# First modulation in two halves of the channels, the loads of the start reordered, and five products in two parts

## The chip, the cores and the metric

One core of one Trainium2 chip runs the whole kernel, one launch of it. The metric is the time on the device in microseconds, the median over runs. Before the change it is 1413.9 us over 3 runs (1413.7 to 1414.58).

## The reference, cut to what matters

A two-layer transformer on 512 tokens of 1024 channels, with a context of 256 tokens. Layer 0 is attention with a mixture of experts, layer 1 a pooling mixer with another one. What the change touches is the beginning of layer 0: a vector of conditions is multiplied by a wide matrix, w_ada (1024 x 6144 per layer), and gives shifts, scales and gates; the normalised input is scaled and shifted by them and goes through one projection to queries, keys and values.

```python
cond_lat, cond_ctx = jax.nn.silu(c), jax.nn.silu(c_ctx)
mod_l = (cond_lat @ w_ada[i] + b_ada[i])[:, None, :]
sh_m, sc_m, g_m, sh_f, sc_f, g_f = jnp.split(mod_l, 6, axis=-1)
h_l = modulate(rms_norm(x_lat, norm_mix_g[i]), sh_m, sc_m)
mc = jnp.split(cond_ctx @ w_ada[i] + b_ada[i], 6)
h_c = modulate(rms_norm(x_ctx, norm_mix_g[i]), mc[0], mc[1])
qkv = h_l @ w_qkv
q_l = rope(rms_norm(q, q_g)); k_l = rope(rms_norm(k, k_g))
kv_c = h_c @ w_qkv[:, 1024:]
```

## The kernel before, in words

Every engine's instructions stand in the order in which the Python code issues them; no scheduler reorders them. The start of the kernel is one function, `project`.

**The stream of weights.** `plan_stream` lists the weight loads in their order, and `Stream.fill` issues them on SyncE's queue (L118) while fewer than `limit` tiles are out and a buffer of the shared pool of 22 is free. `Stream.get` takes a tile, `Stream.done` returns it and fills again. SyncE's queue is one sequence: each load waits for the eighth load before it.

**The first modulation.** The columns 0 to 2047 of w_ada are the shift and the scale of the first norm. They come as eight tiles of 128 rows by 2048 columns, 1 MB each. `ada_part` (L354) multiplies one by the two condition vectors: four matmuls, one for each 512 columns, on the four column groups of TensorE. After 32 of them `ada_rows` holds rows of results (L361), `ada_place` turns them (L441), so that channels lie on partitions, and adds the bias and the norm's gain (L455, L457).

**The normalised input.** `square` and `scale` (L600 to L609) normalise the two context tiles and then the four tiles of x. `h_turn` (L631) turns 128 channels of them on TensorE into a bank, `h_make` applies the modulation on ScalarE (L648) and parts the result in two fp32r numbers, `hi` by a cast on VectorE (L649) and `lo` by a subtraction (L650), on VectorE or POOL by the chunk. `weight_parts` parts the projection's weights in the same way (`split`, L519 on ScalarE and L520 on VectorE or POOL).

**The products.** `seq` has 14 of them, 128 tokens by 512 columns each: 0 and 1 are keys and values of the context, 2 to 5 keys and values of x, 6 to 13 queries. A product is 24 matmuls (`matmul3`, L546): eight chunks of channels by three combinations of parts. Products 0 and 1 need the context's h and the column block 2 of the weights, product 2 all eight chunks of x's h.

**What follows a product.** `others(n)` is called after product n. On VectorE and ScalarE, `turned` takes the norm of product n-1's heads (sum of squares L699, root, several small steps, L702) and applies the rope (L711, with L708 on POOL); between its steps `parted` makes the parts of product n-2's heads (L718, L519, L520), and two steps of `work` part weights of the next column block. Then `place` turns the heads of product n-2 on TensorE (L740), and ScalarE copies them out in the next round (L753). Since TensorE takes its instructions in order, product n+1 stands behind the turns of product n-2, and these behind VectorE's parts.

In the profile `pmm` is a product, `hTc` and `hT` the parts of h for the context and for x, `whl` the parts of the weights, `hl` those of the heads, `ph` the turned input, `pqt` the turned heads, `wt` a tile of the stream.

Of the kernel before, what the change touches and what calls it, by code (L numbers as in the profile page):

```python
# [178 lines left out]
class Kernel:  # L179
# [88 lines left out]
    def plan_stream(self):  # L268
# [12 lines left out]
        ada(0, 0)  # L281
        qkv(2)
# [47 lines left out]
    def cond_columns(self, ps):  # L330
        nc = self.nc
        nc.scalar.activation(self.rowsA[0:16], self.rowsA[0:16], AF.Silu)
        p = ps.tile([128, 512], F32, tag="tr", name="pc")
        nc.tensor.transpose(p[:, :96], self.rowsA, self.ident[:96, :96])
        nc.vector.tensor_copy(self.cols[:, :96], p[:, :96])
        self.cond = self.cp.tile([128, KD, 32], F32, name="cond")
        nc.vector.memset(self.cond, 0.0)
        for c in range(2):
            nc.vector.tensor_copy(self.cond[:, :, c], self.cols[:, 8 * c:8 * c + 8])

# [91 lines left out]
    def ada_place(self, i, b, rows, ps, tag="tr", no_dve=False):  # L432
        nc = self.nc
        eng = nc.gpsimd if no_dve else nc.vector
        if b:
            q = slice(64 * (b - 1), 64 * b)
            eng.tensor_tensor(self.gates[q], self.gates[q], rows[q], op=ALU.add)
        p = ps.tile([128, 512], F32, tag=tag, name="pa")
        pv = p.rearrange("p (n j c) -> p n j c", n=4, c=32)
        for n in range(4):  # L440
            nc.tensor.transpose(p[:, n * 128:(n + 1) * 128], rows[:, n * 128:(n + 1) * 128], self.ident)  # L441
        gains = {1: self.cols[:, 16 + 8 * i:24 + 8 * i], 4: self.cols[:, 32 + 8 * i:40 + 8 * i]}
        tv = lambda z: z.rearrange("p (j n) -> p n j", j=2)
        for m in (2 * b, 2 * b + 1):
            if m in (2, 5):
                continue
            for cond in range(2 if (i == 0 and m < 2) else 1):
                t = self.cp.tile([128, KD], F32, name=f"mod{i}{m}{cond}")
                j0 = 2 * (m % 2)
                bias = self.cols[:, 48 + 48 * i + 8 * m:56 + 48 * i + 8 * m]  # L450
                src = pv[:, :, j0:j0 + 2, cond]
                if no_dve:
                    nc.scalar.copy(tv(t), src)
                    src = tv(t)
                eng.tensor_tensor(tv(t), src, tv(bias), op=ALU.add)  # L455
                if m in gains:
                    nc.vector.scalar_tensor_tensor(t, t, 1.0, gains[m], op0=ALU.add, op1=ALU.mult)  # L457
                self.AB[i, m, cond] = t
# [80 lines left out]
    def matmul3(self, p, lhs, whl, half=None):  # L539

        n = 0
        for k in range(KD):
            if half and k == KD // 2:
                half()
            for pa, pb in ((0, 0), (0, 1), (1, 0)):
                self.nc.tensor.matmul(p, lhs(pa, k), whl[pb, k // 4][:, k % 4], start=(n == 0), stop=(n == 3 * KD - 1))  # L546
                n += 1

    def attention_layer(self, sa):
# [7 lines left out]
        with ExitStack() as s1:  # L557
            self.ps3 = Banks(pool(s1, "psP", 1, space=PSUM), {"mm": 3, "tr": 3})
# [8 lines left out]
    def project(self, s1):  # L567
# [19 lines left out]
        self.gate_biases(0, nc.sync)  # L587
# [22 lines left out]

        js = (4, 5)
# [10 lines left out]
        def h_turn(cond, k):  # L622
# [3 lines left out]
            else:  # L626
                if k % 2 == 0:
                    ph["c"] = ps3.tile([128, 512], F32, tag="mm", name="ph") if k < 6 else ps.tile([128, 512], F32, tag="o", name="ph")
# [5 lines left out]
        def h_make(cond, k):  # L634
# [15 lines left out]
            (nc.vector if k % 4 < 2 else nc.gpsimd).tensor_tensor(lo, h32, hi.bitcast(F32), op=ALU.subtract)  # L650

        for k in range(KD):
            h_turn(1, k)
        for _ in range(4 * KD):
            self.ada_part()
        whl, work = self.weight_parts("qkv", 2, engs=(nc.vector, nc.gpsimd))
        js = range(NT)
        ss = sm.tile([128, NT], F32, name="ss4")
        for _ in range(4):
            work.popleft()()  # L660
        self.ada_end(ps3)
        for part in range(2):
            hT[part, 2] = self.big([128, KD, CTX], F32R, "hTc")
        for z in range(4):
            h_make(1, 2 * z)
            for _ in range((0, 1, 1, 2)[z]):
                work.popleft()()
            if z >= 2:
                square(js, 2 * z - 4, nc.scalar, ss)
                square(js, 2 * z - 3, nc.vector, ss)  # L670
        r = self.rstd_of(ss, NT, D, "n4")
        for j, eng in enumerate((nc.scalar, nc.gpsimd, nc.vector, nc.gpsimd)):
            scale(js, j, eng, r)
# [3 lines left out]
        def product(ch, j, whl, half=None):  # L677

            p = self.ps3.tile([128, 512], F32, tag="mm", name="pmm")
            if j < NT:  # L680
                self.matmul3(p, lambda z, k: hT[z, k // 4][:, k % 4, j * 128:(j + 1) * 128], whl, half)
            else:
                self.matmul3(p, lambda z, k: hT[z, 2][:, k, (j - NT) * 128:(j - NT + 1) * 128], whl, half)
# [71 lines left out]
        def make_tabs():  # L755

            nc.gpsimd.tensor_copy(self.tri_b, rest[:, :128])
            p = ps3.tile([128, 512], F32, tag="tr", name="pc")
            nc.tensor.transpose(p[:, :48], rows1, self.ident[:48, :48])
            nc.vector.tensor_copy(self.cols[:, 96:], p[:, :48])  # L760
            nc.gpsimd.tensor_scalar(gq[:, 0], gq[:, 0], HD ** -0.5, 0.0, op0=ALU.mult, op1=ALU.add)
            for i, n in ((1, "k"), (0, "q")):
                tcs = tabs[n]
                nc.gpsimd.tensor_tensor(tcs[:, 0], rope[:, 0], gq[:, i][:, None, :].to_broadcast([128, NT, HD]), op=ALU.mult)
                for e in range(2):
                    nc.gpsimd.tensor_tensor(tcs[:, 1, :, e::2], rope[:, 1, :, e::2],
                                            gq[:, i, 1 - e::2][:, None, :].to_broadcast([128, NT, HD // 2]), op=ALU.mult)

# [21 lines left out]
        def chunks(turns, makes=()):  # L790
            for k in turns:
                h_turn(0, k)
            for k in makes:
                h_make(0, k)

        work = deque()
        for n, (ch, j) in enumerate(seq):
            if n in (0, 6, 10):
                while work:
                    work.popleft()()  # L800
                whl, (nxt, work) = whl if n == 0 else nxt, self.weight_parts("qkv", 0 if n == 0 else 1) if n < 10 else (None, deque())
            half = {1: lambda: chunks((3, 4, 5), range(3))}.get(n)
            P1[n] = ch, j, product(ch, j, whl, half)
            if n == 0:
                chunks(range(3))
            if n == 1:
                chunks((6, 7), range(3, 8))
                make_tabs()
            others(n, work if n != 1 else None)
# [939 lines left out]
```

## Time and profile before

| | us |
|---|---|
| median of 3 runs | 1413.9 |
| the profiled execution | 1411.9 |
| its span | 1410.1 |
| TensorE busy in it | 1318.7 (94%) |
| VectorE busy | 667.9 (47%) |
| ScalarE busy | 372.7 (26%) |
| GpSimd (POOL) busy | 179.7 (13%) |
| moved by DMA | 474.92 MB, mean 337 GB/s |
| first matmul of product 0 | 35.92 after the span's start |
| first matmul of product 13 | 135.54 |

A timeline row gives an instruction's start, its duration (of all `xcount` merged ones from the first start to the last end), the engine, the line and the operation, tiles as out<-in, and in brackets how long the engine had been idle and what ended that. A window's row gives the busy time of PE, PEld, DVE, ACT and POOL, the granted clock of TensorE as a share of full speed, the DMA engines' busy share, and GB/s. PE is TensorE, PEld its weight load, DVE VectorE, ACT ScalarE, SP SyncE.

### The profile page before, as it was taken

The numbers are of one execution on the slowest core, as the hardware profiler recorded it, in microseconds if no ns is written. First come the engines' busy times: TensorE is split into PE (matmuls) and PEld (weight loads), VectorE is DVE, ScalarE is ACT, GpSimd is POOL, SyncE is SP. The second block draws the span as 40 slices with busy tenths as digits, with TensorE's granted clock in tenths as the row PEclk, the third lists the DMA queues.
The fourth block names the chain that finished last, engine by engine and source line by source line (L and its number), as shares of the span: only waits on it lengthen the run. The fifth ranks groups of instructions, "written<-read, shape, count | busy, mean of one in ns | idle before, by whom it ended". The sixth has DMA issues, their size and how long they took to land. (4 is left out here: it accounts for less than half of the span.)

```text
span 1410.1 us, 18553 instructions
## 1 busy us (share of the span) xinstructions
PE 1318.7 (94%) x7135; PEld 742.5 (53%) x7135; DVE 667.9 (47%) x1241; ACT 372.7 (26%) x713; POOL 179.7 (13%) x159
## 2 busy tenths in 40 slices
PE   4799999998699999999999997779999999999995
PEld 1588677777544554445444444554444544455432
DVE  2777788757433343334342337733433433343325
ACT  2454678744310111111110114511101101011103
POOL 1523254454100000000000014300000000000001
PEclk8899999999899999999999999989999999999998
DMA  9412844178379999999999999458999999999993
GB/s 376 154 61 72 346 156 173 51 266 330 122 286 421 427 426 427 426 426 427 427 426 426 423 417 418 164 198 368 426 426 426 426 427 426 427 427 426 426 420 147
DMA packets 80410, 474.92 MB, mean 337 GB/s; under 512 B 8478, under 2 KB 10030, under 8 KB 30140
## 3 DMA queue, kind: packets, MB, share of 16 engines
q1 hardware_dynamic: 80308, 473.66, 82.0%
q8 instruction: 59, 0.97, 0.3%
q14 instruction: 35, 0.29, 0.1%
q10 hardware_dynamic: 8, 0.01, 0.0%
HBM read 471.54 MB, written 2.10 MB: 336 GB/s over the span
## 5 line engine op out<-in xcount | busy, mean ns | idle before, releaser
L1239 PE MATMUL pgate<-wt,xe 128*64 128x512 f32 x1024 | 264.1, 593 | 0.0
L1239 PE MATMUL pup<-wt,xe 128*64 128x512 f32 x1024 | 263.8, 592 | 0.0
L1264 PE MATMUL py<-wt,aT 128*64 128x512 f32 x960 | 212.6, 595 | 0.0
L1244 DVE TENSOR_TENSOR act<-act,pup 128x512 f32<-128x512 f32 x32 | 22.1, 690 | 335.1 <-ACT act L1243 299.7
L1295 DVE TENSOR_TENSOR x<-x,pc 128x512 f32<-128x512 f32 x240 | 154.1, 683 | 33.0 <-PE pc L1293 33.0
L1222 PE MATMUL pga<-OH,xnp 128*128 128x256 f32 x1024 | 146.5, 290 | 11.1 <-issue 11.1
L1239 PEld LDWEIGHTS pup<-wt,xe 128*64 128x64 f32 x1024 | 74.7, 137 | 145.1 <-issue 144.8
L1222 PEld LDWEIGHTS pga<-OH,xnp 128*128 128x128 f32 x1024 | 138.8, 196 | 19.9 <-issue 12.9
L1239 PEld LDWEIGHTS pgate<-wt,xe 128*64 128x64 f32 x1024 | 74.0, 137 | 142.5 <-issue 132.9
L1293 PE MATMUL pc<-y,scat 128*128 128x512 f32 x480 | 136.6, 405 | 2.5 <-DVE x L1295 2.5
L1277 DVE SCALAR_TENSOR_TENSOR py<-py,r_sw,gw 128x512 f32<-128x512 f32 x64 | 48.6, 759 | 177.4 <-PE py L1264 168.5
L1264 PEld LDWEIGHTS py<-wt,aT 128*64 128x64 f32 x960 | 66.9, 137 | 124.7 <-issue 118.5
L1243 ACT ACTIVATE act<-pgate 128x512 f32<-128x512 f32 x32 | 19.1, 597 | 366.2 <-PE pgate L1239 366.2
L1293 PEld LDWEIGHTS pc<-y,scat 128*128 128x128 f32 x480 | 80.5, 188 | 43.4 <-ACT act L1243 24.3
L1278 ACT ACTIVATE y<-py 128x512 fp32r<-128x512 f32 x64 | 38.2, 597 | 236.8 <-PE py L1264 175.8
L1228 ACT ACTIVATE xe<-pga,mod 128x256 f32<-128x256 f32 x64 | 36.2, 565 | 167.7 <-PE pga L1222 165.3
L546 PE MATMUL pmm<-whl,hT 128*128 128x512 f32 x288 | 70.0, 399 | 0.0
L837 DVE TENSOR_REDUCE mx<-S 128x1 f32<-128x768 f32 x64 | 58.3, 951 | 19.6 <-PE S L834 18.9
L1701 POOL TENSOR_TENSOR xg<-x,gn 128x512 f32<-128x512 f32 x4 | 5.0, 1275 | 479.5 <-DVE x L1327 479.5
L546 PEld LDWEIGHTS pmm<-whl,hT 128*128 128x128 f32 x288 | 54.1, 191 | 11.1
L1226 DVE TENSOR_SCALAR xe<-pga,mod 128x256 f32<-128x256 f32 x64 | 34.8, 544 | 48.3 <-PE pga L1222 44.8
L844 ACT ACTIVATE P<-S,mx 128x768 f32<-128x768 f32 x64 | 57.0, 899 | 2.2 <-POOL rest L718 2.0
(327 smaller groups left out, 1457.5 us busy)
## 6 DMA issues: line engine op xcount, KB each, us to landing
wt<-in_moe_w_gate_up_dram SPq DMA_DIRECT2D x224, 1024.0 KB, 16.1
wt<-in_moe_w_down_dram SPq DMA_DIRECT2D x120, 1024.0 KB, 12.7
wt<-in_w_ada_dram SPq DMA_DIRECT2D x48, 1024.0 KB, 14.2
wt<-in_moe_w_gate_up_dram SPq DMA_DIRECT2D x64, 512.0 KB, 10.3
wt<-in_moe_w_down_dram SPq DMA_DIRECT2D x16, 512.0 KB, 10.5
wt<-in_attn_w_qkv_dram SPq DMA_DIRECT2D x6, 1024.0 KB, 7.4
x<-in_x_dram SPq DMA_DIRECT2D x8, 512.0 KB, 7.9
wt<-in_attn_w_o_dram SPq DMA_DIRECT2D x4, 1024.0 KB, 5.6
```

The costliest lines, as they stand in the source:

```text
L546: self.nc.tensor.matmul(p, lhs(pa, k), whl[pb, k // 4][:, k % 4], start=(n == 0), stop=(n == 3 * KD - 1))
L837: nc.vector.tensor_reduce(m, s[:, :NKEY], axis=AX, op=ALU.max, negate=True)
L844: nc.scalar.activation(P[n][:, g], S.pop((n, g))[:, :NKEY], AF.Exp, bias=mx[n, g], accum_out=total[n // 4][:, 2 * gp + g, kvl:kvl + 1])
L1222: nc.tensor.matmul(p[:, :n], self.parts[part][j // 2][:, j % 2, k * 128:(k + 1) * 128], OH[:, j], start=(z == 0), stop=(z == 2 * NT - 1))
L1226: nc.vector.tensor_scalar(xe, p[:, :n], A[:, k:k + 1], B[:, k:k + 1], op0=ALU.mult, op1=ALU.add)
L1228: nc.scalar.activation(xe, p[:, :n], AF.Identity, bias=B[:, k:k + 1], scale=A[:, k:k + 1])
L1239: nc.tensor.matmul(p[64 * e:64 * e + 64], xe(k)[:, off + 64 * e:off + 64 * e + 64], w[e][:, h * 512:(h + 1) * 512], start=(k == 0), stop=( ...
L1264: nc.tensor.matmul(py[h][64 * e:64 * e + 64], aT[:, j, 64 * e:64 * e + 64], wd[e][:, h * 512:(h + 1) * 512], start=(j == 0), stop=(j == 3) ...
L1277: nc.vector.scalar_tensor_tensor(py, py, w, gf[:, h * 512:(h + 1) * 512], op0=ALU.mult, op1=ALU.mult)
L1278: nc.scalar.activation(y[:, 0], py, AF.Copy)
L1293: nc.tensor.matmul(p, P[:, j * 128:(j + 1) * 128], y[:, part], start=(part == 0), stop=(part == 1))
L1295: nc.vector.tensor_add(xs, xs, p)
```

## The change

The order of the loads: x, rope tables and norm gains come right after the context, then half of the first weights, then w_ada in two halves, then the other half of the weights. A half of w_ada holds 512 channels of the shift and the same 512 of the scale. It is loaded as four tiles of 256 rows, each by two loads of 512 KB. `first_part` gives the four column groups to shift and scale, and to the two sets of 128 rows of a tile; a half has 16 matmuls. `first_turned` adds the two sums in its turn, by a matrix `pairs` of two stacked identities, and writes the modulation of four chunks of channels.

Five products (0 to 4) are computed in two parts: chunks 0 to 3 after the first half of the modulation, chunks 4 to 7 after the second, each into its own bank for so long. The banks of `mm` are four instead of three, those of `tr` two instead of three; product 4 uses the bank `o`. The squares and scales of x, the tables (`make_tabs`) and the first turns of x are issued ahead of w_ada's matmuls. `lo` parts of h and the parts of the first weights are all made on VectorE. `others` for products 0 to 4 is called one product later, and both `others(4)` and `others(5)` after product 5. `ada_place` loses the loop over the two conditions, `make_tabs` moves within `project` unchanged.

```diff
@@ plan_stream
-        ada(0, 0)
-        qkv(2)
+        def ada_half(z):
+            for q in range(4):
+                rows = a["w_ada"][0][q * 256:(q + 1) * 256, :2048].rearrange("(s p) (m h n) -> s p m h n", s=2, m=2, h=2)
+                st.add([rows[s, :, :, z] for s in range(2)], [128, 2, 2, 512], ("ada0", z, q))
...
+        qkv_half(2, 0)
+        for z in range(2):
+            ada_half(z)
+        qkv_half(2, 1)
         qkv(0)
@@ new
+    def first_part(self, z, q):
+        nc = self.nc
+        if q == 0:
+            self.first_ps = self.ps.tile([128, 512], F32, tag="ada", name="ada_ps")
+        w = self.st.get("ada0", z, q)
+        for s in range(2):
+            for m in range(2):
+                j = 2 * m + s
+                nc.tensor.matmul(self.first_ps[32 * j:32 * j + 32], self.cond[:, 2 * q + s], w[:, s, m], start=(q == 0),
+                                 stop=(q == 3), tile_position=(0, 32 * j))
+        self.st.done()
+        if q == 3:
+            self.first_rows = self.sm.tile([128, 512], F32, name="ada_rows", bufs=1)
+            nc.vector.tensor_copy(self.first_rows[:, :256], self.first_ps[:, :256])
+            nc.scalar.copy(self.first_rows[:, 256:], self.first_ps[:, 256:])
+    def first_turned(self, z):
+        nc = self.nc
+        if z == 0:
+            self.pairs = self.cp.tile([128, 2, 2], F32, name="pairs")
+            v = self.ident.rearrange("p (m s c) -> p m s c", m=2, s=2)
+            nc.vector.tensor_tensor(self.pairs, v[:, :, 0, :2], v[:, :, 1, :2], op=ALU.add)
+        p = self.ps3.tile([128, 512], F32, tag="tr" if z else "mm", name="pa")
+        pv = p[:, :16].rearrange("p (n m c) -> p n m c", n=4, m=2)
+        for n in range(4):
+            nc.tensor.matmul(p[:, 4 * n:4 * n + 4], self.first_rows[:, n * 128:(n + 1) * 128], self.pairs.rearrange("p m c -> p (m c)"),
+                             start=True, stop=True)
+        h = slice(4 * z, 4 * z + 4)
+        for cond in (1, 0):
+            for m in range(2):
...
+                t = self.AB[0, m, cond][:, h]
+                nc.vector.tensor_tensor(t, pv[:, :, m, cond], self.cols[:, 48 + 8 * m:56 + 8 * m][:, h], op=ALU.add)
+                if m:
+                    nc.vector.scalar_tensor_tensor(t, t, 1.0, self.cols[:, 16:24][:, h], op0=ALU.add, op1=ALU.mult)
@@ attention_layer
-            self.ps3 = Banks(pool(s1, "psP", 1, space=PSUM), {"mm": 3, "tr": 3})
+            self.ps3 = Banks(pool(s1, "psP", 1, space=PSUM), {"mm": 4, "tr": 2})
@@ project: the loads
-        self.ada_begin(ps, 0, 0)
-        st.fill(KD + 2)
         self.load_x()
-        st.limit = 3
         nc.sync.dma_start(rest[:, :128 + 2 * NT * HD], a["consts"][:, _C["tri"][0]:_C["sin"][1]])
...
+        st.fill(10)
+        st.limit = 3
+        self.gate_biases(0, nc.sync)
         self.load_late_consts()
@@ project: h_make
-            (nc.vector if k % 4 < 2 else nc.gpsimd).tensor_tensor(lo, h32, hi.bitcast(F32), op=ALU.subtract)
+            nc.vector.tensor_tensor(lo, h32, hi.bitcast(F32), op=ALU.subtract)
@@ project: before the products
+        for j in range(NT):
+            square(js, j, (nc.scalar, nc.vector)[j % 2], ss)
+        for k in range(4):
+            h_turn(1, k)
+        r = self.rstd_of(ss, NT, D, "n4")
+        for j, eng in enumerate((nc.scalar, nc.vector, nc.vector, nc.scalar)):
+            scale(js, j, eng, r)
...
+        whl, work = self.weight_parts("qkv", 2)
+        for _ in range(4):
+            work.popleft()()
+        make_tabs()
+        for k in range(2):
+            h_turn(0, k)
+        for q in range(4):
+            self.first_part(0, q)
@@ project: the products
+        half = {}
+        self.first_turned(0)
+        h_make(1, 0)
+        h_make(1, 2)
+        for k in range(2):
+            h_make(0, k)
+        half[0] = product(*seq[0], whl, ks=range(4))
+        for k in range(2, 4):
+            h_turn(0, k)
+            h_make(0, k)
+        half[1] = product(*seq[1], whl, ks=range(4))
+        self.first_part(1, 0)
+        self.first_part(1, 1)
+        half[2] = product(*seq[2], whl, ks=range(4))
+        self.first_part(1, 2)
+        self.first_part(1, 3)
+        half[3] = product(*seq[3], whl, ks=range(4))
+        self.first_turned(1)
+        for k in range(4, KD):
+            h_turn(1, k)
+        half[4] = product(*seq[4], whl, ps.tile([128, 512], F32, tag="o", name="pmm"), range(4))
+        work.popleft()()
+        for k in (4, 6):
+            h_make(1, k)
+            work.popleft()()
+        work.popleft()()
+        nxt, work = self.weight_parts("qkv", 0)
         for n, (ch, j) in enumerate(seq):
...
+            P1[n] = ch, j, product(ch, j, whl, half[n], range(4, KD)) if n in half else product(ch, j, whl)
+            if n < 2:
+                for k in (4 + 2 * n, 5 + 2 * n):
+                    h_turn(0, k)
+                for k in (4 + 2 * n, 5 + 2 * n):
+                    h_make(0, k)
+            for m in (n - 1,) if n < 5 else (4, 5) if n == 5 else (n,):
+                if m >= 0:
+                    others(m, work if n > 1 else None)
```

SyncE's queue after the context's load and the small rows, before the change (`wt` from w_ada or the projection's weights, `rest` the rope tables and the second layer's biases):

```order
L118 DMA wt<-in_w_ada_dram 128x2048 x8
L118 DMA wt<-in_attn_w_qkv_dram 128x4x512 x2
L222 DMA x<-in_x_dram 128x1024 x4
L585 DMA rest<-in_consts_dram 128x640
L586 DMA rest<-in_b_ada_dram 48x128
```

The same place in the change:

```order
L222 DMA x<-in_x_dram 128x1024 x4
L628 DMA rest<-in_consts_dram 128x640
L629 DMA rest<-in_b_ada_dram 48x128
L631 DMA gq<-in_attn_q_norm_g_dram 128x64
L631 DMA gq<-in_attn_k_norm_g_dram 128x64
L118 DMA wt<-in_attn_w_qkv_dram 128x4x512
L118 DMA wt<-in_w_ada_dram 128x2x512 x16
L118 DMA wt<-in_attn_w_qkv_dram 128x4x512
```

x, the tables, the gains and half of the weights have moved ahead of w_ada, and eight loads of it have become sixteen.

TensorE from the first modulation to the turns of the first heads, before the change (each row of 24 or 12 is a product or a half of one):

```order
L354 MATMUL ada_ps<-wt,cond 32x512 x32
L441 MATMUL pa<-cst,ada_rows 128x128 x4
L546 MATMUL pmm<-whl,hTc 128x512 x24
L631 MATMUL ph<-cst,xn 128x128 x12
L546 MATMUL pmm<-whl,hTc 128x512 x12
L631 MATMUL ph<-cst,xn 128x128 x12
L546 MATMUL pmm<-whl,hTc 128x512 x12
L631 MATMUL ph<-cst,xn 128x128 x8
L759 MATMUL pc<-cst,rest 128x48
L546 MATMUL pmm<-whl,hT 128x512 x24
L740 MATMUL pqt<-ident_r,hl 128x128 x8
```

The same place in the change, from the first product on:

```order
L593 MATMUL pmm<-whl,hTc 128x512 x12
L690 MATMUL ph<-cst,xn 128x128 x8
L593 MATMUL pmm<-whl,hTc 128x512 x12
L362 MATMUL ada_ps<-wt,cond 32x512 x8
L593 MATMUL pmm<-whl,hT 128x512 x12
L362 MATMUL ada_ps<-wt,cond 32x512 x8
L593 MATMUL pmm<-whl,hT 128x512 x12
L380 MATMUL pa<-pairs,ada_rows 128x4 x4
L690 MATMUL ph<-cst,xn 128x128 x8
L593 MATMUL pmm<-whl,hT 128x512 x12
L593 MATMUL pmm<-whl,hTc 128x512 x12
```

The second half of the modulation's matmuls now stands between first halves of products 1 to 4.

TensorE in the change from the last turns of x on, through products 2 to 6:

```order
L690 MATMUL ph<-cst,xn 128x128 x8
L593 MATMUL pmm<-whl,hT 128x512 x24
L797 MATMUL pqt<-ident_r,hl 128x128 x8
L593 MATMUL pmm<-whl,hT 128x512 x12
L797 MATMUL pqt<-ident_r,hl 128x128 x8
L593 MATMUL pmm<-whl,hT 128x512 x24
L797 MATMUL pqt<-ident_r,hl 128x128 x16
L593 MATMUL pmm<-whl,hT 128x512 x24
```

The first row of 24 here is the second halves of products 2 and 3, the row of 12 that of product 4. Before product 6 stand the turned heads of two products, where every other product has those of one ahead of it.

## Rows read from the trace of the kernel before

**Rows 1.** The page, part 2: TensorE, granted clock, and DMA rate in 40 slices.

```profile
PE   4799999998699999999999997779999999999995
...
GB/s 376 154 61 72 346 156 173 51 266 330 122 286 421 427 426 427 426 426 427 427 426 426 423 417 418 164 198 368 426 426 426 426 427 426 427 427 426 426 420 147
```

**Rows 2.** Windows of 5 us: busy by engine, clock, DMA share, GB/s.

```profile
20.00:25.00 5.00, 2.18 (x24) 0.32 (x16) 0.00 (x0) 0.00 (x0) 0.00 (x0) 1.00 1.01 428
...
30.00:35.00 5.00, 1.05 (x4) 0.65 (x4) 3.40 (x8) 2.62 (x6) 2.94 (x2) 0.50 1.04 419
...
40.00:45.00 5.00, 3.96 (x14) 2.37 (x12) 4.89 (x8) 2.21 (x5) 2.89 (x3) 0.93 1.04 397
```

**Rows 3.** Windows of 1 us, columns as in rows 2.

```profile
38.00:39.00 1.00, 1.00 (x3) 0.77 (x3) 0.96 (x2) 1.00 (x2) 1.00 (x2) 0.50 0.94 193
74.00:75.00 1.00, 1.00 (x5) 0.77 (x4) 0.89 (x3) 0.05 (x1) 0.00 (x0) 0.58 0.00 0
```

**Rows 4.** Timeline of PE, the start: start us, us, line, operation, count, [idle before <-releaser].

```profile
16.04 4.86 PE L354 MATMUL ada_ps<-wt,cond 128*32 128x512 f32 x40
...
27.20 1.93 PE L354 MATMUL ada_ps<-wt,cond 128*32 128x512 f32 x8 [1.34 <-DMA wt<-in_w_ada_dram]
29.94 1.11 PE L441 MATMUL pa<-cst,ada_rows 128*128 128x128 f32 x4 [0.81 <-DVE ada_rows L361]
35.92 7.30 PE L546 MATMUL pmm<-whl,hTc 128*128 128x512 f32 x20 [4.87 <-DVE hTc L649]
...
60.33 1.03 PE L631 MATMUL ph<-cst,xn 128*128 128x128 f32 x8
```

**Rows 5.** Timeline of ACT, the making of h.

```profile
34.30 1.94 ACT L648 ACTIVATE h<-ph,mod,mod 128x256 f32<-128x256 f32 x4 [2.38 <-DVE mod L457]
...
51.23 2.48 ACT L648 ACTIVATE h<-ph,mod,mod 128x512 f32<-128x512 f32 x3 [1.68 <-PE ph L631]
```

**Rows 6.** Timeline of DVE, a modulation column's last step, one pair of parts of h.

```profile
34.04 0.17 DVE L457 SCALAR_TENSOR_TENSOR mod<-mod,cols 128x8 f32<-128x8 f32 x1
35.35 0.43 DVE L649 CAST hTc<-h 128x512 fp32r<-128x512 f32 x1 [1.15 <-ACT h L648]
35.81 0.69 DVE L650 TENSOR_TENSOR hTc<-h,hTc 128x512 fp32r<-128x512 f32 x1
```

**Rows 7.** Timeline of PE, products and turned heads.

```profile
70.64 0.54 PE L740 MATMUL pqt<-ident_r,hl 128*128 128x128 f32 x4 [3.40 <-ACT hl L519]
...
71.97 7.05 PE L546 MATMUL pmm<-whl,hT 128*128 128x512 f32 x24
...
91.86 5.73 PE L546 MATMUL pmm<-whl,hT 128*128 128x512 f32 x24
...
123.15 5.73 PE L546 MATMUL pmm<-whl,hT 128*128 128x512 f32 x24
```

**Rows 8.** Timeline of DVE, the norms of the products: each L699 opens one product's.

```profile
63.95 0.40 DVE L699 TENSOR_REDUCE ssh<-sq 128x4 f32<-128x256 f32 x1
...
69.21 0.41 DVE L699 TENSOR_REDUCE ssh<-sq 128x4 f32<-128x256 f32 x1
...
70.61 0.69 DVE L520 TENSOR_TENSOR hl<-q,hl 128x512 fp32r<-128x512 f32 x1 [0.79 <-ACT hl L519]
...
85.70 0.42 DVE L699 TENSOR_REDUCE ssh<-sq 128x4 f32<-128x256 f32 x1 [0.15 <-ACT sq L692]
...
87.69 0.70 DVE L520 TENSOR_TENSOR hl<-q,hl 128x512 fp32r<-128x512 f32 x1 [1.03 <-ACT hl L519]
...
91.90 0.42 DVE L699 TENSOR_REDUCE ssh<-sq 128x4 f32<-128x256 f32 x1 [1.71 <-ACT sq L692]
...
98.31 0.69 DVE L699 TENSOR_REDUCE ssh<-sq 128x8 f32<-128x512 f32 x1 [0.41 <-ACT sq L692]
...
119.42 0.67 DVE L699 TENSOR_REDUCE ssh<-sq 128x8 f32<-128x512 f32 x1
...
121.69 0.69 DVE L520 TENSOR_TENSOR hl<-q,hl 128x512 fp32r<-128x512 f32 x1 [0.76 <-ACT hl L519]
```

More of the change, by code (lines that the diff above doesn't have):

```diff
@@ L446, in ada_place @@
                 continue
[L447 to L458, printed above, removed]
+            t = self.cp.tile([128, KD], F32, name=f"mod{i}{m}")
+            j0 = 2 * (m % 2)
+            bias = self.cols[:, 48 + 48 * i + 8 * m:56 + 48 * i + 8 * m]
+            src = pv[:, :, j0:j0 + 2, 0]
+            if no_dve:
+                nc.scalar.copy(tv(t), src)
+                src = tv(t)
+            eng.tensor_tensor(tv(t), src, tv(bias), op=ALU.add)
+            if m in gains:
+                nc.vector.scalar_tensor_tensor(t, t, 1.0, gains[m], op0=ALU.add, op1=ALU.mult)
+            self.AB[i, m, 0] = t
     def row_bcast(self, bank, m, g, eng=None):
@@ L537, in weight_parts, with matmul3 @@
         return whl, deque(lambda h=h, k=k: step(h, k) for h in range(2) for k in range(4))
[L539 to L547, printed above, removed]
+    def matmul3(self, p, lhs, whl, ks=range(KD)):
+        for k in ks:
+            for n, (pa, pb) in enumerate(((0, 0), (0, 1), (1, 0))):
+                self.nc.tensor.matmul(p, lhs(pa, k), whl[pb, k // 4][:, k % 4], start=(k + n == 0), stop=(k == KD - 1 and n == 2))
     def attention_layer(self, sa):
@@ L609, in scale, with make_tabs @@
                 eng.tensor_scalar(o, x, r[:, n:n + 1], 0.0, op0=ALU.mult, op1=ALU.add)
+        def make_tabs():
+            nc.gpsimd.tensor_copy(self.tri_b, rest[:, :128])
+            p = ps3.tile([128, 512], F32, tag="tr", name="pc")
+            nc.tensor.transpose(p[:, :48], rows1, self.ident[:48, :48])
+            nc.vector.tensor_copy(self.cols[:, 96:], p[:, :48])
+            nc.gpsimd.tensor_scalar(gq[:, 0], gq[:, 0], HD ** -0.5, 0.0, op0=ALU.mult, op1=ALU.add)
+            for i, n in ((1, "k"), (0, "q")):
+                tcs = tabs[n]
+                nc.gpsimd.tensor_tensor(tcs[:, 0], rope[:, 0], gq[:, i][:, None, :].to_broadcast([128, NT, HD]), op=ALU.mult)
+                for e in range(2):
+                    nc.gpsimd.tensor_tensor(tcs[:, 1, :, e::2], rope[:, 1, :, e::2],
+                                            gq[:, i, 1 - e::2][:, None, :].to_broadcast([128, NT, HD // 2]), op=ALU.mult)
         js = (4, 5)
@@ L664, in project @@
[L664 to L673, printed above, removed]
+        make_tabs()
+        for k in range(2):
+            h_turn(0, k)
@@ L675, in project, with product @@
+        for q in range(4):
+            self.first_part(0, q)
         heads = lambda z: z.rearrange("p (h d) -> p h d", d=HD)
-        def product(ch, j, whl, half=None):
-            p = self.ps3.tile([128, 512], F32, tag="mm", name="pmm")
+        def product(ch, j, whl, p=None, ks=range(KD)):
+            p = p or self.ps3.tile([128, 512], F32, tag="mm", name="pmm")
             if j < NT:
-                self.matmul3(p, lambda z, k: hT[z, k // 4][:, k % 4, j * 128:(j + 1) * 128], whl, half)
+                self.matmul3(p, lambda z, k: hT[z, k // 4][:, k % 4, j * 128:(j + 1) * 128], whl, ks)
@@ L788, in others @@
                 place(*P3.pop(min(P3)))
[L790 to L796, printed above, removed]
+        half = {}
[25 more added lines that the diff above has]
+        nxt, work = self.weight_parts("qkv", 0)
         for n, (ch, j) in enumerate(seq):
-            if n in (0, 6, 10):
+            if n in (6, 10):
                 while work:
                     work.popleft()()
[L801 to L809, printed above, removed]
+                whl, (nxt, work) = nxt, self.weight_parts("qkv", 1) if n < 10 else (None, deque())
+            P1[n] = ch, j, product(ch, j, whl, half[n], range(4, KD)) if n in half else product(ch, j, whl)
[7 more added lines that the diff above has]
+                    others(m, work if n > 1 else None)
         N = len(seq)
```

32 lines of the change are left out of this document (9 added, 23 removed).

## The prediction

> **What bounds the kernel now.** The page comes first. TensorE is busy nine tenths or more from slice 2 on, and from slice 12 the DMA rate lies at 418 to 427 GB/s wherever experts run [rows 1]. Neither is full in three places: slices 9 and 10 (routing) and 24 to 27 (the pooling layer and its routing), which the change leaves alone, and the first 2 slices, some 70 us, which it rewrites. So the windows and the timelines of the first 150 us are what I read next, engine by engine, to see which wait ends last there.
>
> Until 27.20 us the start waits for memory: w_ada's eight tiles arrive at 428 GB/s [rows 2], TensorE gets the last at 27.20, and the chain rows, turn, modulation, h, parts takes until the first product at 35.92 [rows 4]. The clock has fallen meanwhile: that product runs at half clock and takes 7.30 us for 20 matmuls. The third product can begin only when x has arrived and been normalised, turned and parted.
>
> From 63.95 on the other thing to see is VectorE [rows 8]. Each product gives it a norm, a rope, two parts of the heads and, in most steps, two parts of the next weights; the row L699 opens a product's share. Ten shares lie between 63.95 and 119.42, 55.5 us, and VectorE is idle for want of a product in only three spots: 0.15 before 85.70, 1.71 before 91.90, 0.41 before 98.31. TensorE has 24 matmuls (5.73) and 8 turns per product [rows 7], 6.2 to 6.4 together; a share with eight heads and two weight parts costs VectorE some 7.1. The two engines are nearly matched, TensorE a little behind. That decides this case: an earlier start helps only as far as both chains can follow.
>
> **The loads.** Moved: x, rope and the two gains now stand ahead of w_ada, one half of the first weights too. Before, 9 MiB of context and w_ada had landed at 27.20. Now the first half of w_ada is complete after 1 (context) + 2 (x) + 0.31 (rope) + 1 (weights) + 4 = 8.31 MiB. That is 0.69 MiB less, 1.7 us at 2.45 us per MiB. Against it: the weights and w_ada now come in pieces of 512 columns, and a stretch of such weights ran at 397 GB/s instead of 428 [rows 2], 0.19 us per MiB, 0.95 for five. The small loads, which now lie ahead, ran at 193 GB/s in their microsecond [rows 3]: 0.6. Sum: 27.20 - 1.7 + 0.95 + 0.6 = 27.05. The first half lands when the whole did. The second lands four MiB (10.6) later, at 37.6; it is wanted later still, as follows.
>
> Each w_ada load is now 512 KB, sixteen instead of eight. x's loads have that size, and their window shows 419 GB/s [rows 2], so I charge nothing for size. [...]
>
> **From landing to the first product.** The last two matmuls of a half: 1.0 (half of 1.93, at half clock). The row copy is split over two engines: 0.55 instead of 0.81. The turn has as many matmuls as before, 1.11, and only 16 columns come out; the stationary rows are as large, so I keep 1.11. Bounds: 0.3 and 1.11. Three steps on VectorE for the context's modulation at 0.2 (0.17 and the gap) and 0.15 for the hand-over: 0.75. Two ScalarE halves at 0.485 (1.94 / 4): 1.0 [rows 5]. The cast, 0.43 and a hand-over [rows 6]: 0.45. 27.05 + 4.9 = 32.0, against 35.92. The start is 3.9 us earlier.
>
> **TensorE from there to the third product.** The order is fixed, so this is a sum: five first halves of products, 12 matmuls or 2.85 each (half of 5.7), 14.25; two second halves, 5.7; 16 matmuls of the second half of w_ada, 3.9 (20 in 4.86 [rows 4]); 32 turns of h at 0.13 (8 in 1.03), 4.1; the second turn, warm, 0.6; a wait of 0.8, since the turns of context chunks 6 and 7 need the bank that the second modulation is read from; 2.0 for a cold start (20 matmuls in 7.30 instead of 4.75 is 2.55 for all of it; the clock should rise some 4 us in). Together 31.35. Then the last two chunks of x are made and parted, 2 x (0.83 + 1.12) overlapped over two engines and with the turn of the first: 2.6. VectorE opens the first product's share at 32.0 + 31.35 + 2.6 = 65.95. That is 2.0 **later** than the 63.95 of before, though TensorE has by then three products and two halves behind it instead of two and most of one. Bounds: 63.5 (no cold start, no wait) and 68.5 (cold until the fifth half).
>
> The parts that POOL made (two pairs for the context, four for x, four weight parts) go to VectorE: 10 x 0.69 = 6.9. They lie under TensorE's sum, where VectorE then has 12 pairs at 1.12, four weight parts at 0.69, 12 modulation steps at 0.2 and two copies, 19.5 us in 34. If that cover is gone they cost up to 6.9. Tables and the normalising of x move under the loads and cost nothing: VectorE's window from 20 to 25 shows 0.00 busy [rows 2]. Without that cover the last three steps of x's norm would cost some 3 us.
>
> **VectorE from there.** The ten shares have the same instructions as before. From the 55.5 come off the idle spots 0.15, 1.71, 0.41, and 0.8 in the first share (5.26 before, with table work of POOL beside it and without weight parts; 4.5 now, without the one and with the other). 52.4: the eleventh share opens at 118.35, before 119.42. **1.1 earlier**, with no idle left.
>
> **TensorE beside it.** It runs ahead of VectorE at once: the second halves of products 3 and 4 take 2.85 each, a share 4.5 to 5.8. After product 5 it must place the heads of products 2 and 3 before product 6. Product 3's parts end 2.7 us into its step's share (85.70 to the end of the row at 87.69) [rows 8], and that share opens at 65.95 + 20.8 = 86.75 (85.70 - 63.95, less 0.15 and 0.8); with the last four turns product 6 starts at 90.15, against 91.86. TensorE has stood for 4 to 5 us by then. Before, after 3.40 us of standing, the clock was low again, 0.58 in the last microsecond of it [rows 3], and the product took 7.05 instead of 5.73 [rows 7]. So 1.3 comes back. From product 6 to product 11 before: 123.15 - 91.86 = 31.3, of which 0.2 is a wait for parts that end at 122.38 [rows 8]. Product 11 starts at 90.15 + 31.1 + 1.3 = 122.55, **0.6 earlier**; VectorE alone would allow 119.42 to 121.69 and 0.69 more [rows 8] and a turn after 118.35, 122.0. TensorE's 0.6 decides. From product 11 on no weight parts are left for VectorE, TensorE is the bound in both kernels, and the 0.6 stays: the attention layer's loads wait for buffers that the products free, so they move along, and so does the expert stream, which starts when its ring may be filled.
>
> **Sum.** 3.9 gained at the start and some 10 us of product work drawn forward; nearly all of it meets a VectorE chain that opens 2.0 later. The profiled execution took 1411.9, 2.0 under the median of 1413.9; with 0.6 off, 1411.3, and the median 1413.3. About 0.2%, 2.8 us, is what a measurement of this kernel tells from no change, so the forecast is **no change**, own range 1410.8 to 1415.9 (VectorE's opening at 63.5 makes it 3.1 faster, at 68.5 it is 2.0 slower).
>
> **Rivals.** *VectorE is not the bound.* Then TensorE runs on from 65.95: two second halves 5.7, nine products 51.6, twelve placings at 0.64, 7.7: product 13 ends at 131 instead of 141.3, 10 us faster, 1403.6. For: TensorE's sum. Against: rows 8, ten shares without a gap. Something between, 3 to 8 us faster, needs an opening before 63.5 or shares that shrink where POOL is idle. Chance of faster 0.23, of which 0.08 for the whole 10 us.
>
> *The first half lands late.* Pieces of 2 KB from rows 24 KB apart may run slower than the weights did. Each us after 27.7 is a us lost, since everything behind it hangs on that landing; from 30.5 the kernel is slower by over 2.8. At 300 GB/s, between 193 [rows 3] and 397, five MiB take 17.5 instead of 13.2: VectorE opens at 70.2, 3.7 slower, 1417.6. For: no load of this shape is in the trace. Against: x's size and the weights' pieces each cost little. A cover lost on VectorE (6.9 at most) gives the same sign. The extreme is that each load runs by itself: at 193 GB/s a half takes 21.7 instead of 10.6, 1424; 0.02. [...] Chance of slower 0.15 with it.
>
> *The change doesn't do what it says*, if half products wait for their parts: VectorE gives a chunk of x in 1.12 and TensorE uses one in 0.71 or, cold, more. Five halves would then end later, but not before the second half of w_ada is used; that is inside the own range, 0.05 of its chance. Within 0.2%: 0.62.
>
> **Range.** 1409.4 to 1416.8: it leaves out about 1 in 10 on the fast side and somewhat under that on the slow side.
>
> **What would show it.** The first w_ada half used up near 28; first product at 32; VectorE's first L756 (the former L699) at 66, and the following ones with no idle ended by ScalarE's squares; a stand of TensorE of 4 us or more before product 6, with the clock at half after it; product 11 within 1 us of 123. Wrong it is if VectorE opens before 63, if TensorE doesn't stand there, or if the first product starts after 35.

## The result, and the profile after

The changed kernel takes 1426.36 us (median of 4 runs, 1424.92 to 1427.01) against 1413.8 for the kernel before beside it: 1.0092 times as long, 95% interval 1.008 to 1.0105. It is **12.6 us slower**; no change was forecast, and the time lies outside the range. The profiled execution took 1424.92, span 1422.9, against 1410.1.

The view to begin with is one that the change doesn't touch. First the DMA rate in the 40 slices of the page after (counted from 0), to be laid beside [rows 1]:

```profile
GB/s 338 188 59 79 335 175 153 55 262 325 120 327 421 419 419 421 418 420 419 419 419 419 413 404 411 165 208 366 419 420 419 420 419 419 420 419 419 419 412 169
```

Up to slice 12 the two rows differ in both directions or not at all. From slice 13 on every slice that ran at 426 or 427 runs at 418 to 421. A window of 100 us shows the same with nothing else changed. The kernel before:

```profile
600.00:700.00 100.00, 100.00 (x521) 50.81 (x518) 38.72 (x66) 12.76 (x22) 0.00 (x0) 1.00 1.01 427
```

The changed kernel, in the last row; the two rows above it are of its start and come up again below:

```profile
10.00:15.00 5.00, 2.42 (x9) 1.72 (x9) 4.22 (x14) 3.43 (x6) 0.91 (x1) 1.00 0.77 295
...
25.00:30.00 5.00, 4.72 (x28) 0.98 (x20) 0.00 (x0) 0.00 (x0) 0.00 (x0) 1.00 1.04 387
...
600.00:700.00 100.00, 100.00 (x522) 50.98 (x518) 38.70 (x66) 12.89 (x22) 0.00 (x0) 1.00 1.01 419
```

In the window from 600 us clock and DMA share are the same, only the bytes per second are not. SyncE's queue says when the loss begins. Its timeline (SPq, loads of the experts' weights) in the kernel before:

```profile
496.74 5.76 SPq L118 DMA_DIRECT2D wt<-in_moe_w_down_dram  x3
```

and in the changed one:

```profile
496.57 5.76 SPq L118 DMA_DIRECT2D wt<-in_moe_w_down_dram  x3
```

At 497 us the changed kernel is 0.17 ahead; at the end it is 12.8 behind. So 13.0 us go after the stage that was rewritten. Slices 14 to 24 and 28 to 38, 22 of 35.25 us, have rates that add up to 9187 against 9352 before; 775 us of stream at 1.8% less come, as an estimate, to 13.9, the size of the whole loss. TensorE's weight loads wait for it: the two rows are the wait of the gate's weight loads for a tile of the stream from 480 us on (us in total, times, longest), in the kernel before and in the changed one:

```profile
PEld pgate L1239 <- DMA wt<-in_moe_w_gate_up_dram: 0.5, 2, 0.3
```

```profile
PEld pgate L1306 <- DMA wt<-in_moe_w_gate_up_dram: 13.2, 20, 1.2
```

**The start** can be read by itself. TensorE's timeline, as [rows 4, 7], and three of VectorE's shares, as [rows 8]. The profile counts each of w_ada's matmuls twice, so x28 are 14 of a half's 16:

```profile
22.51 1.11 PE L690 MATMUL ph<-cst,xn 128*128 128x128 f32 x4 [2.63 <-DVE cols L661]
23.55 5.33 PE L362 MATMUL ada_ps<-wt,cond 128*32 128x512 f32 x28
29.16 1.05 PE L362 MATMUL ada_ps<-wt,cond 128*32 128x512 f32 x4 [0.28 <-DMA wt<-in_w_ada_dram]
...
33.90 4.58 PE L593 MATMUL pmm<-whl,hTc 128*128 128x512 f32 x12 [2.03 <-DVE hTc L708]
...
88.90 1.47 PE L797 MATMUL pqt<-ident_r,hl 128*128 128x128 f32 x8 [3.91 <-ACT hl L569]
90.17 8.12 PE L593 MATMUL pmm<-whl,hT 128*128 128x512 f32 x24
...
123.86 5.71 PE L593 MATMUL pmm<-whl,hT 128*128 128x512 f32 x24
```

```profile
66.54 0.41 DVE L756 TENSOR_REDUCE ssh<-sq 128x4 f32<-128x256 f32 x1
...
99.02 0.69 DVE L756 TENSOR_REDUCE ssh<-sq 128x8 f32<-128x512 f32 x1 [1.57 <-ACT sq L749]
...
120.12 0.67 DVE L756 TENSOR_REDUCE ssh<-sq 128x8 f32<-128x512 f32 x1
```

First product at 33.90 (forecast 32.0, before 35.92), VectorE opens at 66.54 (65.95), TensorE stands 3.91 before product 6 (4 to 5), and that product is long, 8.12. VectorE then waits 1.57 for ScalarE's squares, and its tenth share opens at 120.12, 0.70 after the 119.42 of [rows 8], where 118.35 was forecast. So this stage came out within 2 us of the forecast, and it isn't where 12.6 us went.

### The profile page after: what moved, and what is told of

It reads as the page before. It is cut to its first block, busy times and chain, and to the rows that moved or that the text cites. A ratio compares the mean times of both kernels' runs of the same rounds, so it can differ in the third digit from the quotient of the medians.

```text
span 1422.9 us, 18589 instructions
## 1 busy us (share of the span) xinstructions
PE 1328.9 (93%) x7147; PEld 743.0 (52%) x7147; DVE 666.5 (47%) x1260; ACT 374.6 (26%) x716; POOL 163.1 (11%) x147
## 5 line engine op out<-in xcount | busy, mean ns | idle before, releaser
L1306 PE MATMUL pgate<-wt,xe 128*64 128x512 f32 x1024 | 281.2, 594 | 1.4 <-DMA wt<-in_moe_w_gate_up_dram 1.3
L1306 PE MATMUL pup<-wt,xe 128*64 128x512 f32 x1024 | 279.0, 593 | 0.0
L1306 PEld LDWEIGHTS pgate<-wt,xe 128*64 128x64 f32 x1024 | 77.6, 137 | 152.3 <-issue 129.7
L1306 PEld LDWEIGHTS pup<-wt,xe 128*64 128x64 f32 x1024 | 78.5, 137 | 145.1 <-issue 144.5
L1289 PEld LDWEIGHTS pga<-OH,xnp 128*128 128x128 f32 x1024 | 138.2, 195 | 20.8 <-issue 13.9
```

The lines of the kernel that those rows point to most:

```text
L1289: nc.tensor.matmul(p[:, :n], self.parts[part][j // 2][:, j % 2, k * 128:(k + 1) * 128], OH[:, j], start=(z == 0), stop=(z == 2 * NT - 1))
L1306: nc.tensor.matmul(p[64 * e:64 * e + 64], xe(k)[:, off + 64 * e:off + 64 * e + 64], w[e][:, h * 512:(h + 1) * 512], start=(k == 0), stop=( ...
```

## The experiments

**The theory and its rival.** What the change adds for the rest of the program is one small tile: `pairs`, 16 bytes in each partition, allocated in the constants' pool and given 32. Everything allocated later moves up by 32 bytes, the 22 buffers of 8 KB of the shared pool among it, into which the weight stream is loaded: they began at byte 30208 of each partition, a multiple of 256, and now at 30240. The theory is that this start slows every DMA into them. The rival is that the new order of the loads at the start leaves the stream in another phase, or that the half products disturb it later. The same buffers also hold what TensorE reads in the experts, so a slower engine would be another way; but a matmul of the gate takes 593 ns on average before and 594 after, and its weight load 137 in both.

**1. `pairs` elsewhere.** In the attention layer's own pool, which lies behind the ring:

```diff
-            self.pairs = self.cp.tile([128, 2, 2], F32, name="pairs")
+            self.pairs = self.ap.tile([128, 2, 2], F32, name="pairs")
```

> The changed kernel with the 16-byte tile pairs in the attention layer's pool instead of the pool of constants, so that the 22 ring buffers begin at byte 30208 of a partition (a multiple of 512) as before the change, and not at 30240. Theory A (the ring's start, 32 bytes off, lowers the rate of every load): DMA in the experts is back at 426 to 427 GB/s from 419, and the time falls from 1426 to that of before give or take 2 us (1411 to 1416). Rival B (the sixteen loads of 512 KB and their order leave a slower pattern in the queue): nothing changes, 1424 to 1428 and 419 GB/s. Rival C (the rate belongs to the build or the chip): any value, and not in step with the next three runs.

1412.39 against 1412.55, ratio 0.9996 (0.9987 to 1.0005). Its windows:

```profile
25.00:30.00 5.00, 5.00 (x28) 0.98 (x20) 0.00 (x0) 0.00 (x0) 0.00 (x0) 1.00 1.05 408
...
600.00:700.00 100.00, 100.00 (x522) 50.95 (x520) 39.23 (x67) 12.89 (x22) 0.00 (x0) 1.00 1.01 427
```

The stream is back at 427 GB/s. The rows of 2 KB of w_ada, in the window from 25 us, come at 408 where the change had 387.

**2. The shift without the change.** A tile that is written once and never read, in the constants' pool of the kernel before; 8, 16, 32 or 64 columns put the ring 32, 64, 128 or 256 bytes up:

```diff
+        nc.vector.memset(cp.tile([128, 8], F32, name="pad"), 0.0)
```

> The kernel before with a tile of 32 bytes more among the constants, written once by VectorE, so that the ring begins at 30240; nothing of the change is in it. Theory A: 419 GB/s in the experts and 1424 to 1427 us. Rival B: 427 GB/s and 1414. Rival C: any value.

> The kernel before with 64 bytes more, ring at 30272: a multiple of 64, not of 128. Theory A in its narrow form (only a start off a multiple of 64 costs): 427 GB/s and 1414. Theory A in its wide form (a start off a multiple of 256 or 512 costs): 419 to 424 GB/s and 1417 to 1426. Rival B: 1414.

> The kernel before with 256 bytes more, ring at 30464: a multiple of 256, not of 512. Theory A narrow: 427 GB/s, 1414. Theory A wide: 1414 if 256 is what counts, slower if 512 is. Rival B: 1414.

> The kernel before with 128 bytes more among the constants, ring at 30336: a multiple of 128, not of 256. If every start off a multiple of 256 costs: 419 to 425 GB/s in the experts and 1416 to 1424 us. If only a start off a multiple of 128 costs: 426 to 427 GB/s and 1413.

| ring starts at | shift | median | ratio to before | 95% | window 600 to 700, GB/s |
|---|---|---|---|---|---|
| 30240 | 32 | 1427.28 | 1.0101 | 1.0085 to 1.0116 | 419 |
| 30272 | 64 | 1423.8 | 1.0074 | 1.0059 to 1.0089 | 421 |
| 30336 | 128 | 1423.27 | 1.0062 | 1.0047 to 1.0078 | 421 |
| 30464 | 256 | 1413.4 | 1.0004 | 0.9995 to 1.0013 | 426 |

Each ratio is to the kernel before as it ran beside that shift. The windows of the shifts by 32, 64, 128 and 256, one after another:

```profile
600.00:700.00 100.00, 100.00 (x519) 50.53 (x516) 38.39 (x66) 12.32 (x22) 0.00 (x0) 1.00 1.01 419
```

```profile
600.00:700.00 100.00, 100.00 (x517) 50.13 (x514) 37.70 (x65) 12.29 (x21) 0.00 (x0) 1.00 1.01 421
```

```profile
600.00:700.00 100.00, 100.00 (x516) 49.95 (x513) 37.65 (x65) 12.29 (x21) 0.00 (x0) 1.00 1.01 421
```

```profile
600.00:700.00 100.00, 100.00 (x521) 50.86 (x518) 38.68 (x66) 12.79 (x22) 0.00 (x0) 1.00 1.01 426
```

An empty tile of 32 bytes alone makes the kernel before as slow as the change is, and moving `pairs` away takes all of it back. So the cause is where the ring starts, and the rival falls. Of the starts tried, those on a multiple of 256 lose nothing (427 GB/s at 30208, 426 at 30464) and those on a multiple of 32, 64 or 128 alone do: 1.9% with the shift of 32 (427 to 419), 1.4% with those of 64 and 128 (421); 512 isn't needed (30464 is no multiple of it). Only the address on the chip moved in these runs, so it is the written side whose start counts here. What in the chip makes the difference no run shows.

**3. What holds the aligned version back.** The rest starts from experiment 1's kernel. In it the start's rows are these, TensorE's and VectorE's timelines:

```profile
23.82 6.22 PE L362 MATMUL ada_ps<-wt,cond 128*32 128x512 f32 x32
...
33.73 4.80 PE L593 MATMUL pmm<-whl,hTc 128*128 128x512 f32 x12 [2.03 <-DVE hTc L708]
...
90.21 6.71 PE L593 MATMUL pmm<-whl,hT 128*128 128x512 f32 x24
...
122.51 5.70 PE L593 MATMUL pmm<-whl,hT 128*128 128x512 f32 x24
...
134.86 5.69 PE L593 MATMUL pmm<-whl,hT 128*128 128x512 f32 x24
```

```profile
66.60 0.41 DVE L756 TENSOR_REDUCE ssh<-sq 128x4 f32<-128x256 f32 x1
...
118.77 0.67 DVE L756 TENSOR_REDUCE ssh<-sq 128x8 f32<-128x512 f32 x1
...
142.28 0.68 DVE L756 TENSOR_REDUCE ssh<-sq 128x8 f32<-128x512 f32 x1
```

VectorE's last share in the kernel before:

```profile
142.93 0.68 DVE L699 TENSOR_REDUCE ssh<-sq 128x8 f32<-128x512 f32 x1
```

Product 11 starts at 122.51, 0.64 before [rows 7]; the tenth share opens at 118.77, 0.65 before [rows 8], and the last at 142.28 against 142.93. Three edits, alone and then together. *Lag*: the turned heads of each product stay one product later to the end, instead of two sets before product 6.

```diff
-            for m in (n - 1,) if n < 5 else (4, 5) if n == 5 else (n,):
-                if m >= 0:
-                    others(m, work if n > 1 else None)
+            if n:
+                others(n - 1, work if n > 1 else None)
...
+        others(N - 1, None)
```

> The changed kernel with pairs moved, and the call that follows a product kept one product late to the end (the change catches up after product 5). Theory (VectorE's chain of ten shares is the bound in the start, and TensorE's stand of 4 us before product 6 comes from the catching up): the stand goes, product 13 ends near 133 instead of 140.5, but VectorE's last share opens at 140 instead of 142.3, so 1 to 3 us faster than a_pairs_moved, 1409.5 to 1411.5. Rival (TensorE's stand itself is what is lost, 4 us and its cold clock): 5 to 8 us faster, 1404.5 to 1407.5. Rival (the end waits for the extra call after the last product): no faster, or slower by up to 3.

1414.31, ratio 1.0002 (0.9994 to 1.0011): no faster, where 1 to 3 us were expected. TensorE's and VectorE's timelines:

```profile
129.35 5.69 PE L593 MATMUL pmm<-whl,hT 128*128 128x512 f32 x24
...
146.26 1.25 PE L797 MATMUL pqt<-ident_r,hl 128*128 128x128 f32 x8 [5.16 <-DVE hl L570]
```

```profile
136.39 0.68 DVE L756 TENSOR_REDUCE ssh<-sq 128x8 f32<-128x512 f32 x1
...
138.02 0.69 DVE L775 TENSOR_TENSOR q<-q,q 128x512 f32<-128x512 f32 x1 [0.75 <-POOL q L765]
139.47 0.69 DVE L570 TENSOR_TENSOR hl<-q,hl 128x512 fp32r<-128x512 f32 x1 [0.76 <-ACT hl L569]
...
142.46 0.68 DVE L756 TENSOR_REDUCE ssh<-sq 128x8 f32<-128x512 f32 x1
```

TensorE gets ahead, product 13 at 129.35 instead of 134.86, but VectorE's last share still opens at 142.46, its shares 6.08 each at the end with waits for POOL and ScalarE in them, and TensorE then stands 5.16. So what is won on TensorE alone doesn't come through: 6.08 is also what the last shares take in the kernel before (136.85 to 142.93).

*Pool*: four of the second weights' eight parts go to POOL (the new index keeps the other four on VectorE).

```diff
-            self.split(whl[h][:, k], whl[0, h][:, k], whl[1, h][:, k], engs[k % len(engs)])
+            self.split(whl[h][:, k], whl[0, h][:, k], whl[1, h][:, k], engs[(4 * h + k) % len(engs)])
...
-        nxt, work = self.weight_parts("qkv", 0)
+        nxt, work = self.weight_parts("qkv", 0, engs=(nc.gpsimd,) * 4 + (None,) * 4)
```

> The changed kernel with pairs moved, and four of the eight parts of the second weights made on POOL, those in the first two shares, where POOL has nothing else. Theory (VectorE's chain is the bound): its chain is 4 x 0.69 shorter, less what POOL's work slows it; product 6 starts 1.5 to 2.8 us earlier and the time falls as much, to 1409.6 to 1411. Rival (TensorE is the bound): nothing, 1412.4 give or take 0.8.

1413.15, ratio 0.9999 (0.999 to 1.0007): nothing, and product 6 starts at 90.24 where it started at 90.21. That is the number of the rival, but not its reason, as the timelines show. Timelines of POOL and, beside it, of VectorE:

```profile
66.91 2.53 POOL L570 TENSOR_TENSOR whl<-wt,whl 128x512 fp32r<-128x512 f32 x2 [47.99 <-ACT whl L569]
72.34 2.52 POOL L570 TENSOR_TENSOR whl<-wt,whl 128x512 fp32r<-128x512 f32 x2 [2.90 <-ACT whl L569]
```

```profile
66.75 0.16 DVE L546 TENSOR_TENSOR h4t<-h4t,h4v 128x4 f32<-128x4 f32 x1
66.95 1.29 DVE L547 TENSOR_SCALAR h4t<-h4t 128x4 f32<-128x4 f32 x1
68.27 1.19 DVE L548 TENSOR_TENSOR h4r<-h4r,h4t 128x4 f32<-128x4 f32 x1
...
72.38 0.17 DVE L543 RECIPROCAL h4r<-h4r 128x4 f32<-128x4 f32 x1
72.59 1.05 DVE L545 TENSOR_TENSOR h4t<-h4r 128x4 f32<-128x4 f32 x1
73.68 1.20 DVE L546 TENSOR_TENSOR h4t<-h4t,h4v 128x4 f32<-128x4 f32 x1
```

Four small steps of the root, 0.16 to 0.17 each in experiment 1, where POOL does nothing from 65 to 77 us, take 1.05 to 1.29, and each ends within 0.1 of the end of one of POOL's parts (1.26 each). VectorE's first two shares became 4.92 and 5.82 where they were 4.49 and 5.09, although two parts of 0.69 had left each.

*Loads*: the small loads follow the first half of w_ada, and the tables are made after `first_part(1, 1)`.

```diff
+        st.fill(5)
...
-        make_tabs()
...
+        make_tabs()
```

> The changed kernel with pairs moved, and the four small loads (rope tables, biases, two gains) issued after the first half of w_ada instead of before the first weights; the tables are made later. Theory (those loads hold SyncE's queue, so that the memory stood idle for over 1 us at 10 to 15 us, DMA share 0.77): the first product starts 1.5 to 2.5 us before 33.73, VectorE opens as much before 66.6, and the time falls by 1 to 2 us, to 1410.4 to 1411.4. Rival (all of the start is hidden behind VectorE's chain or lost to a cold clock): under 0.5 us, 1412.

1411.0, ratio 0.998 (0.9971 to 0.9989): a gain of 0.2%, as expected. Window, TensorE and VectorE:

```profile
10.00:15.00 5.00, 2.15 (x8) 1.54 (x8) 4.22 (x14) 3.43 (x6) 0.00 (x0) 1.00 1.02 394
```

```profile
19.90 4.04 PE L362 MATMUL ada_ps<-wt,cond 128*32 128x512 f32 x24
...
25.49 1.05 PE L362 MATMUL ada_ps<-wt,cond 128*32 128x512 f32 x4 [0.26 <-DMA wt<-in_w_ada_dram]
...
30.66 0.73 PE L593 MATMUL pmm<-whl,hTc 128*128 128x512 f32 x2 [2.47 <-DVE hTc L709]
```

```profile
63.85 0.41 DVE L756 TENSOR_REDUCE ssh<-sq 128x4 f32<-128x256 f32 x1
...
139.50 0.68 DVE L756 TENSOR_REDUCE ssh<-sq 128x8 f32<-128x512 f32 x1
```

The queue stays full (394 GB/s instead of the change's 295 and the 266 of experiment 1), the half is used up at 26.5, the first product comes 3.1 and VectorE's first share 2.75 earlier, and the last share 2.8 earlier: what VectorE's opening gains goes through to the end. *All* three together:

> The three edits of a_lag, a_pool and a_loads together. If each shortens the chain that decides (VectorE from its opening at 66.6 on), they add up: 5 to 7 us faster than a_pairs_moved, 1405.5 to 1407.5, and faster than the kernel before by over 0.2%. If TensorE becomes the bound in between, 3 to 5: 1407.5 to 1409.5.

1412.1, ratio 0.9994 (0.9984 to 1.0003), worse than the loads alone, where 5 to 7 us of gain were expected; the last share opens at 141.13, 1.6 after that of the loads alone. The three don't add up. Which of the other two spoils the loads' gain was not followed further.

**4. Shorten VectorE's chain instead.** The loads' edit, and the eight parts of the second weights, which stand in VectorE's first four shares, are made while TensorE does the first halves:

```diff
+        st.fill(7)
+        st.limit = 3
...
+        nxt, early = self.weight_parts("qkv", 0)
+        for _ in range(4):
+            early.popleft()()
...
-        nxt, work = self.weight_parts("qkv", 0)
+        for _ in range(4):
+            early.popleft()()
+        work = deque()
```

> a_loads, and the second weights loaded right behind the first, so that their eight parts are made where VectorE still has nothing to do (four before the second modulation, four before the last chunks of x) and no longer in the first four shares. Theory (VectorE's chain from its opening on is the bound, and the last shares take 6.1 us each whatever TensorE does): the first four shares lose 8 x 0.69 = 5.5 less 1.5 of waits that the parts had filled; VectorE's last share opens 2 to 4 us before the 139.50 of a_loads, and the time falls to 1406 to 1409. Rival (buffers: the loads wait for slots and hold TensorE): no faster than a_loads, 1411 or more.

**1404.86** against 1413.82, ratio 0.9941 (0.9928 to 0.9955): faster than both kernels, and somewhat more than was expected (1406 to 1409). VectorE and TensorE:

```profile
63.89 0.41 DVE L758 TENSOR_REDUCE ssh<-sq 128x4 f32<-128x256 f32 x1
...
79.00 0.41 DVE L758 TENSOR_REDUCE ssh<-sq 128x4 f32<-128x256 f32 x1
...
134.96 0.68 DVE L758 TENSOR_REDUCE ssh<-sq 128x8 f32<-128x512 f32 x1
```

```profile
81.27 0.54 PE L799 MATMUL pqt<-ident_r,hl 128*128 128x128 f32 x4 [1.84 <-ACT hl L569]
...
82.55 7.06 PE L593 MATMUL pmm<-whl,hT 128*128 128x512 f32 x24
```

The first share opens where it did with the loads alone, the fifth at 79.00 instead of 84.49, the last 4.5 earlier than there and 8.0 earlier than before; TensorE's stand before product 6 shrinks to 1.84.

## Why the prediction was wrong

**The step that failed** is the end of the prediction's part on TensorE: "the attention layer's loads wait for buffers that the products free, so they move along, and so does the expert stream". It took the rate of the stream, 418 to 427 GB/s in [rows 1], as a constant of the kernel. The runs show that the rate depends on where the buffers lie: 419 instead of 427, and 13.0 us lost after 497 us. The change moves them by a tile, `pairs`, that the prediction never names and so puts at nothing. None of its rivals has this mechanism. The slower ones were of the start, and the start costs under 1 us. Nor did any of its three conditions for being wrong come true: they all lie in the start, and none looks at the 775 us of stream behind it.

**VectorE's chain as the bound: right in the main**, and borne out with the ring where it was. There product 11 came 0.64 earlier, forecast 0.6, and the time didn't change; giving TensorE 5 us (lag) moved nothing; taking 5.5 us of parts out of VectorE's shares (early; 8 of 0.69) brought the end 4.5 forward. The rival that VectorE is no bound falls. The parts' copies on ScalarE left the shares with them, so the runs don't part the two engines; that it is VectorE rests on the busy time, 45.97 of the 56 us from 64 to 120 in experiment 1 against ScalarE's 30.78. Three things in this part were off. Between 63.95 and 119.42 lie nine shares, not ten (119.42 opens the tenth); the sum used the 55.5 us and is not touched. That from product 11 on "TensorE is the bound in both kernels" isn't borne out: in lag product 13 starts 5.5 us earlier and the last shares still take 6.08. And "no idle left" held in experiment 1 (0.15) but not in the change, where the long product 6 cost VectorE 1.57.

**The first half of w_ada: too small.** Its last load was there at 29.16, where the wait for DMA ends, instead of 27.05, and used up at 30.2 instead of 28. The sum lacks two causes. From 10 to 15 us the queue ran at 295 GB/s and a DMA share of 0.77; with the small loads behind the half it ran at 394. The term of 0.6 stood for one slow microsecond; 295 instead of 394 over these 5 us is, as an estimate, 1.3. That the small loads make this hole the edit shows: from 13 to 14 us the change has a DMA share of 0.21 and 60 GB/s, with them behind it is 1.06 and 408. SyncE's queue shows a load waiting for the eighth before it: w_ada's sixth is issued at 15.49 after a wait for the first gain's, eight places ahead, which went at 7.82 and took 7.7 to land. That the small loads make the hole by the places they take there is argued. The second cause is the place of the ring once more: 387 GB/s from 25 to 30 us where 397 was charged and experiment 1 has 408, as an estimate 0.3 us more than charged for the 5 MiB. Less the 0.6 that was charged, the two make up about half of the 2.1; the rest stays open. The matmuls' own late start, at 23.55 behind a turn of x that waited for VectorE until 22.51, did not set the end, since TensorE caught up and waited 0.28 for the last load; with the tables moved they began at 19.90. **From there to the first product: right**, 4.74 (29.16 to 33.90) against 4.9.

**TensorE until VectorE opens: right** in sum, 32.6 (33.90 to 66.54) against 33.95. The cold start in it is right too: the granted clock was 0.50 from 34 to 37 us, and the first half of product 0 took 4.58 where a warm one was put at 2.85, 1.7 of the 2.0 charged. That VectorE opened only 0.6 after the forecast is luck: the first product was 1.9 late, and 1.3 of it came back here. **Cold product 6**: the stand was 3.91, forecast 4 to 5; the product took 8.12, forecast 7.05 as in [rows 7]. The granted clock was 0.50 from 89 to 95 us and 1.00 from 96 on; in experiment 1, after a stand of 3.90, it was 0.50 from 89 to 92 and the product took 6.71. Why it stayed low for longer in one of them no run shows. The long product put product 11 at 123.86 instead of 122.55. In experiment 1 product 11 came within 0.04 of the forecast, which is luck in part as well: VectorE opened 0.65 late there, and product 6 was 0.34 shorter than charged.

**Pieces of 512 KB**: with the ring where it was, a half's loads ran at 408 GB/s (25 to 30 us), against 397 charged and the 428 of the loads of 1 MB before. Whether the difference from 428 is the size of a load or its rows of 2 KB the runs don't part. The rival in which each load runs by itself falls.

## What to carry to other kernels

A new tile, however small, moves the buffers allocated after it, as the 16 bytes of `pairs` moved the ring by 32: look at what lies behind it, and lay buffers that DMA fills on multiples of 256 bytes, where this kernel lost nothing (426 to 427 GB/s against 419 to 421 from the other starts tried). After a change read the DMA rate in a stretch that the change doesn't touch before explaining anything in the one that it does. Where two engines are nearly matched, take work from the one whose idle spots are gone, into a stretch where it is idle; in these runs work drawn forward on the other one only made it wait.

## What was unexpected of the hardware

Rows of 8 KB per partition, in the window from 600 us, land at 426 to 427 GB/s from the two starts tried on a multiple of 256 bytes, at 419 from the one that is 32 off, at 421 from those 64 and 128 off, all at the same DMA share of 1.01. Rows of 2 KB lose more: 387 instead of 408 with the start 32 off, 5%. Worked out from these figures, with the load spread evenly over the 16 DMA engines that the page counts, a row of 8 KB takes some 6 ns more and a row of 2 KB some 4, so the estimate is that the price goes by the row rather than by the byte; only one start was tried with the short rows.

Steps of VectorE on 128 x 4 elements, 0.16 to 0.17 each in experiment 1, take up to 1.29 beside POOL's subtractions of 1.26 and end with them. Of those with two inputs, the ones at 68.27, 72.59 (the same tile twice) and 73.68 take 1.19, 1.05 and 1.20. Of those with one input the reciprocal at 72.38 takes its 0.17 while POOL works, but the one at 66.95 takes 1.29. What makes the difference no run shows.
